# Second feed-forward and MLP with 128-column weight blocks as the stationary operand

## The chip, the core and the metric

The kernel runs on one core of a Trainium2 chip. The metric is the device time of one execution in microseconds; the median of several runs is given. A core has five engines that run their own instruction queues in order: TensorE (PE in the profile, with its weight loads as PEld), VectorE (DVE), ScalarE (ACT), GpSimd (POOL) and SyncE (SP), and 16 DMA engines.

## The reference

Two blocks of a transformer follow each other, on 256 tokens of 1024 features, in fp32. The part that the change touches is the gated feed-forward of the first block's second layer and the MLP of the second block:

```python
def swiglu(h, w_in, w_out):                 # D_FF = 2816
    g, u = jnp.split(h @ w_in, 2, axis=-1)
    return (jax.nn.silu(g) * u) @ w_out

x = layer_norm(ALPHA * x + g2 * swiglu(modulate(x, sh2, sc2), ffn_w_in[i], ffn_w_out[i]), ...)
...
h2 = rms_norm(x, norm_mlp[i])               # D_FF_2 = 4096
x = x + jnp.square(jax.nn.relu(h2 @ w_up[i])) @ w_down[i]
ple_gate = jax.nn.sigmoid(rms_norm(x, norm_ple[i]) @ w_ple_gate[i])
x = x + ple_gate * (p[i] @ w_ple[i])
```

## The kernel before

Tokens stand in two halves (t = 0, 1) of 128. Products are made from fp32 numbers that are split in two fp32r parts: hi is the number rounded to fp32r, lo the rest; a product is hi·hi + hi·lo + lo·hi. The transposed activations of a stage stand in `xTh` (hi) and `xTl` (lo), 128 features by 8 k by 256 tokens.

All weights come as tiles of 128 x 1024 in the order of one list (`make_plan`). SP issues one DMA per tile into a ring of 11 raw tiles. `Stream.split` turns a raw tile into hi (ACT, L285) and lo (DVE, L291). Eight split tiles can be held. `st.done(key)` gives a tile back and `pump` then issues the next split, as long as fewer than 7 are held; `st.get` of a tile that isn't split yet issues it in any case, as the eighth. Each engine's instructions run in the order in which the program issues them (`manual_schedule`), so where a split, an evacuation or a norm is issued sets its place in its engine's queue.

The layer's second feed-forward, `ffn(1, ...)`, takes its 2816 inner columns in chunks of 512 (one of 256): for each chunk and half, `do_g` and `do_u` multiply with the activations as the stationary operand and 512 weight columns moving (`mmN`, L376 to L378), into a PSUM tile of `mmt()`; ACT applies Silu (L961), DVE multiplies (L969). `tr` transposes the result in 128 x 128 pieces on PE (L981), because the output product needs the inner features on the partitions, and `split_evac` makes hh (ACT, L425) and hl (DVE, L426) of it. `o` multiplies these with the O weights into `ops_[t]` (`mmK`, L390 and L392; the last chunk in `mmK_tail`, L403 to L405). The MLP does the same with `up`, `trm` (L1603) and `down`, ReLU on ACT (L1595) and the square on DVE (L1596), in 8 chunks of 512.

At the start of a phase only the first token half is ready. In the feed-forward `x1_ready` is called within `do_u(0, 0)`: it transposes s[1] (L722), ACT scales it per feature in 128-column pieces (L745) and splits it (L425, L426). In the MLP `rx_t(1, ...)` is called behind `up(0, 0)`: L722, then eight scalings on ACT (L736) and eight on DVE (L738). Both chains begin with a norm that is issued ahead of the phase (`ln_core`, L890; `rms_core`, L1214 to L1219). At the end of a phase `after0` or `rcore(0)` computes the norm of half 0 while PE still multiplies for half 1, and in the MLP `rx_t(0, ...)` transposes it ahead of the last 24 matmuls. `mid` holds steps of the next stage (rows, modulation columns) that are issued within the chunks.

PSUM tiles: two each of `mmt`, `trt` (one bank) and `big` (two banks).

Of the kernel before, what the change touches and what calls it, by code (L numbers as in the profile page):

```python
# [10 lines left out]
F32R = mybir.dt.float32r  # L11
# [7 lines left out]
P = 128  # L19
# [44 lines left out]
UPM = 8  # L64
# [12 lines left out]
def nblocks(key, src, row0, rows, col0, width):  # L77
    per = BW // width
    return [("w", key + (i,), src, row0 + i * per * P, per, col0, width) for i in range(rows // (per * P))]


def make_plan():
# [43 lines left out]
    f1 = ffn(1)  # L126
# [13 lines left out]
    prev = []  # L140
    for j in range(DMLP // 512):
        plan += nblocks(("UP", j), ("w_up_2", 0), 0, D, 512 * j, 512) + prev
        prev = [("w", ("DN", j, i), ("w_down_2", 0), 512 * j + i * P, 1, 0, 1024) for i in range(4)]
    plan += prev
# [27 lines left out]
def body(ctx: ExitStack, tc: tile.TileContext, wst, prm, cst, cst2, poolp, xT_d, cT_d, x_d, head, lam_d,  # L172
# [51 lines left out]
    xTh = cp.t([P, KD, T], "xTh", F32R)  # L224
    xTl = cp.t([P, KD, T], "xTl", F32R)
# [184 lines left out]
    def xlh(t):  # L410
        return lambda k: (xTh[:, k, t * P:(t + 1) * P], xTl[:, k, t * P:(t + 1) * P])

# [729 lines left out]

    pps = [big()]
# [95 lines left out]
    ffn(1, fp, x_t(1), ac1(0), lambda: None, after1_1, {XM: mid_xa, 4: mid1_c, 5: mid_g2r})  # L1239
# [345 lines left out]
    J = DMLP // 512  # L1585
    hs, hT = {}, {}
    ops_ = [big(), big()]

    def up(j, t, mid={}):
        ps = mmt()  # L1590
        mmN(ps, xlh(t), mkey(("UP", j), 4), mid=mid)
        if t == 1:
            st.done(*mkey(("UP", j), 4))
        h = fp.t([P, 512], f"h{t}", bufs=2)
        A.activation(h, ps, AF.Relu)  # L1595
        V.tensor_tensor(h, h, h, op=OP.mult)  # L1596
        hs[j, t] = h

    def trm(j, t):
        h = hs.pop((j, t))  # L1600
        ps = trt()
        for i in range(4):
            TE.transpose(ps[:, i * P:(i + 1) * P], h[:, i * P:(i + 1) * P], ident)  # L1603
        hh = fp.t([P, 4, P], f"hh{t}", F32R, bufs=2)
        hl = fp.t([P, 4, P], f"hl{t}", F32R, bufs=2)
        split_evac(ps.rearrange("p (k t) -> p k t", t=P), hh, hl)
        hT[j, t] = (hh, hl)

    def down(j, t, done):
        hh, hl = hT.pop((j, t))  # L1610
        if j == J - 1:
            keys = [("DN", j, i) for i in range(4)]
            mmK_tail(halves(ops_[t]), [(hh[:, i], hl[:, i]) for i in range(4)], keys)
# [5 lines left out]
        for i in range(4):  # L1619
            mmK(halves(ops_[t]), (hh[:, i], hl[:, i]), ("DN", j, i), j == 0 and i == 0, False)  # L1620
            if done:
                st.done(("DN", j, i))
# [147 lines left out]
```

## Time and profile before

| | |
|---|---|
| median of 3 runs | 1156.6 us (1154.83 to 1158.38) |
| profiled execution | 1158.82 us, its span 1156.8 us |
| mean granted clock of TensorE | 0.993 |
| PE busy | 1116.0 us (96%), 5186 matmuls |
| DVE, ACT busy | 760.6 us (66%), 558.8 us (48%) |
| weight splits | 316 on ACT (1056 ns) and 316 on DVE (1220 ns) |
| HBM read | 232.6 MB, 202 GB/s over the span |

The span is the time from the first to the last instruction of the profiled execution; the 2.0 us by which its own time is longer lie around it. Matmuls are pipelined and their ends are modelled, so the duration of one (some 390 ns for 512 columns) is longer than the distance between the starts of two. A time in brackets behind an instruction is idle time of its engine just before it, with what ended it.

### The profile page before, as it was taken

The numbers are of one execution on the slowest core, as the hardware profiler recorded it, in microseconds if no ns is written. First come the engines' busy times: TensorE is split into PE (matmuls) and PEld (weight loads), VectorE is DVE, ScalarE is ACT, GpSimd is POOL, SyncE is SP. The second block draws the span as 40 slices with busy tenths as digits, with TensorE's granted clock in tenths as the row PEclk, the third lists the DMA queues.
The fourth block names the chain that finished last, engine by engine and source line by source line (L and its number), as shares of the span: only waits on it lengthen the run. The fifth ranks groups of instructions, "written<-read, shape, count | busy, mean of one in ns | idle before, by whom it ended". The sixth has DMA issues, their size and how long they took to land. (4 is left out here: it accounts for less than half of the span.)

```text
span 1156.8 us, 14163 instructions
## 1 busy us (share of the span) xinstructions
PE 1116.0 (96%) x5186; PEld 881.8 (76%) x5186; DVE 760.6 (66%) x1114; ACT 558.8 (48%) x913; POOL 22.7 (2%) x35
## 2 busy tenths in 40 slices
PE   7999888999999999999999999999999999999998
PEld 3578665678888776888887787886777877888887
DVE  7984967669986875677346765455545785555465
ACT  3452456454444527544444755457235374445353
POOL 0000000000000000000000110000000000000000
PEclk9999989999999999999999999999999999999999
DMA  9972742569997915668563755444344645464611
GB/s 360 351 274 102 273 145 66 196 236 357 354 419 286 336 58 203 218 225 300 170 231 119 241 188 180 146 164 153 102 146 130 216 151 195 166 210 163 206 38 37
DMA packets 65922, 234.62 MB, mean 203 GB/s; under 512 B 7323, under 2 KB 8347, under 8 KB 65852
## 3 DMA queue, kind: packets, MB, share of 16 engines
q1 hardware_dynamic: 64080, 227.97, 55.7%
q10 hardware_dynamic: 1772, 5.74, 1.5%
q8 instruction: 41, 0.67, 0.2%
q14 instruction: 29, 0.24, 0.1%
HBM read 232.63 MB, written 1.05 MB: 202 GB/s over the span
## 5 line engine op out<-in xcount | busy, mean ns | idle before, releaser
L291 DVE TENSOR_TENSOR lo<-raw,hi 128x1024 fp32r<-128x1024 f32 x316 | 375.2, 1220 | 139.8 <-ACT hi L285 136.1
L285 ACT ACTIVATE hi<-raw 128x1024 fp32r<-128x1024 f32 x316 | 322.5, 1056 | 82.9 <-PE mm L378 60.9
L376 PE MATMUL mm<-hi,xTh 128*128 128x512 f32 (+1 forms) x872 | 337.6, 387 | 4.0 <-ACT xTh L425 2.7
L377 PE MATMUL mm<-lo,xTh 128*128 128x512 f32 (+1 forms) x872 | 331.8, 380 | 2.0 <-DVE lo L291 1.3
L378 PE MATMUL mm<-hi,xTl 128*128 128x512 f32 (+1 forms) x872 | 332.2, 381 | 0.6 <-DVE xTl L738 0.4
L376 PEld LDWEIGHTS mm<-hi,xTh 128*128 128x128 f32 x872 | 164.1, 188 | 40.8 <-issue 4.7
L378 PEld LDWEIGHTS mm<-hi,xTl 128*128 128x128 f32 x872 | 164.0, 188 | 34.0 <-DVE xTl L426 1.9
L377 PEld LDWEIGHTS mm<-lo,xTh 128*128 128x128 f32 x872 | 164.2, 188 | 33.5 <-DVE lo L291 3.6
L269 DVE SCALAR_TENSOR_TENSOR raw<-raw,crow 128x1024 f32<-128x1024 f32 x80 | 96.7, 1218 | 0.0
L390 PE MATMUL big<-hi,hh 128*128 128x512 f32 x256 | 80.6, 396 | 0.0
L390 PE MATMUL big<-lo,hh 128*128 128x512 f32 x256 | 79.2, 391 | 0.0
L392 PE MATMUL big<-hi,hl 128*128 128x512 f32 x256 | 79.0, 390 | 0.0
L425 ACT ACTIVATE hh<-tr 128x512 fp32r<-128x512 f32 (+1 forms) x40 | 23.0, 576 | 97.4 <-PE tr L981 54.8
L961 ACT ACTIVATE h<-mm 128x512 f32<-128x512 f32 (+1 forms) x24 | 13.5, 561 | 90.2 <-PE mm L378 90.2
L426 DVE TENSOR_TENSOR hl<-tr,hh 128x512 fp32r<-128x512 f32 (+1 forms) x40 | 26.3, 661 | 46.3 <-ACT hh L425 45.6
L392 PEld LDWEIGHTS big<-hi,hl 128*128 128x128 f32 x256 | 48.1, 188 | 10.4
L390 PEld LDWEIGHTS big<-lo,hh 128*128 128x128 f32 x256 | 48.0, 188 | 10.3
L390 PEld LDWEIGHTS big<-hi,hh 128*128 128x128 f32 x256 | 46.7, 188 | 8.6
L420 POOL TENSOR_TENSOR st<-st,half 128x4 f32<-128x4 f32 (+1 forms) x28 | 21.8, 778 | 1036.8 <-DVE st L418 1023.6
L1596 DVE TENSOR_TENSOR h<-h 128x512 f32<-128x512 f32 x16 | 11.0, 688 | 33.6 <-ACT h L1595 33.5
L1595 ACT ACTIVATE h<-mm 128x512 f32<-128x512 f32 x16 | 9.6, 599 | 38.0 <-PE mm L378 38.0
L667 ACT ACTIVATE p<-big,st 128x512 f32<-128x512 f32 x16 | 11.0, 689 | 31.7 <-DVE st L666 31.7
(316 smaller groups left out, 1261.5 us busy)
## 6 DMA issues: line engine op xcount, KB each, us to landing
raw<-in_dram SPq DMA_DIRECT2D x426, 512.0 KB, 5.0
row<-in_dram ACTq DMA_DIRECT2D x8, 512.0 KB, 6.4
tok<-in_dram SPq DMA_DIRECT2D x8, 256.0 KB, 7.5
xa<-in_dram SPq DMA_DIRECT2D x2, 512.0 KB, 5.7
out_dram<-sg SPq DMA_DIRECT2D x3, 256.0 KB, 2.0
pmat<-in_dram ACTq DMA_DIRECT2D x1, 544.0 KB
crow<-in_dram ACTq DMA_DIRECT2D x1, 512.0 KB, 6.8
out_dram<-sg SPq DMA_DIRECT2D x2, 128.0 KB, 1.7
```

The lines of the kernel that those rows point to most:

```text
L269: V.scalar_tensor_tensor(raw, raw, 1.0, crow, op0=OP.mult, op1=OP.mult, accum_out=mc[l][:, nb:nb + 1])
L285: A.activation(hi, raw, AF.Copy)
L291: V.tensor_tensor(lo, raw, hi.bitcast(F32), op=OP.subtract)
L376: TE.matmul(ps, h, hi[:, sl], start=s, stop=False)
L377: TE.matmul(ps, h, lo[:, sl], start=False, stop=False)
L378: TE.matmul(ps, l, hi[:, sl], start=False, stop=e)
L390: TE.matmul(halves[f], h, w[:, f * 512:(f + 1) * 512], start=first and b == 0, stop=False)
L392: TE.matmul(halves[f], l, hi[:, f * 512:(f + 1) * 512], start=False, stop=last)
L420: G.tensor_tensor(r, v, half_e[:, :w], op=OP.pow)
L425: A.activation(dh, ps, AF.Copy)
L426: V.tensor_tensor(dl, ps, dh.bitcast(F32), op=OP.subtract)
L961: A.activation(h[:, :w], ps[:, :w], AF.Silu)
```

## The change

Weight blocks of 128 inner columns become the stationary operand and the activations move, so that the inner activations come out with features on the partitions. `xTh` and `xTl` become one tile `xT4` in which, for each k, the 256 tokens of hi lie beside those of lo. `ws_mm` issues per k one matmul of the hi weights on both parts (512 columns) and one of the lo weights on the hi part (256 columns) into the lo half of the PSUM tile; `ws_sum` adds the two halves (a copy on ACT, an addition on DVE). The transposes are gone; `split_evac` now reads the result from SBUF. `ws_order` writes out the order: the first 3 blocks (feed-forward) or 4 (MLP) run for token half 0, then x1 is called, then they run for half 1; all later blocks run for both halves at once, and output products follow at least two blocks (lag) behind, except that the last 7 blocks' products for half 1 are kept for the end. The four last blocks' products are in `tail`. `ws_plan` lists the weight tiles in the order of use, and the three steps of `mid` move to blocks 6, 16 and 19 of 22.

```diff
--- before.py
+++ after.py
@@ -61,7 +61,7 @@
 XR = (6, 6)
 MQ = 6
 BA = 6
-UPM = 8
+WM = (6, 16, 19)
 F32K = (0, 1, 2, 3, 4)
 VM = (1, 1, 1, 1, 0, 0, 0, 0)
 EN = (0, 2, 0)
@@ -77,6 +77,35 @@
 def nblocks(key, src, row0, rows, col0, width):
     per = BW // width
     return [("w", key + (i,), src, row0 + i * per * P, per, col0, width) for i in range(rows // (per * P))]
+
+
+def ws_order(n, n0, lag, keep_):
+
+    seq = [("in", i, 0) for i in range(n0)] + [("x1", 0, 0)] + [("in", i, 1) for i in range(n0)]
+    q = 0
+    for i in range(n0, n):
+        seq.append(("in", i, None))
+        while q <= min(i - lag, n - 6):
+            seq += [("out", q, t) for t in range(1 if q >= n - keep_ else 2)]
+            q += 1
+    seq += [("out", i, 0) for i in range(q, n - 4)] + [("tail", n - 4, 0), ("a0", 0, 0)]
+    seq += [("out", i, 1) for i in range(n - keep_, n - 4)] + [("m1", 0, 0), ("tail", n - 4, 1), ("a1", 0, 0)]
+    return seq
+
+
+WS_F = (DFF // P, 3, 2, 7)
+WS_M = (DMLP // P, 4, 2, 7)
+
+
+def ws_plan(order, ins, outs):
+    plan, seen = [], set()
+    for kind, i, t in ws_order(*order):
+        fs = {"in": [ins(i)], "out": [[outs(i)]], "tail": [[outs(j) for j in range(i, i + 4)]]}.get(kind, [])
+        for b in sum(fs, []):
+            if b[1] not in seen:
+                seen.add(b[1])
+                plan.append(b)
+    return plan
 
 
 def make_plan():
@@ -123,7 +152,8 @@
     f0 = ffn(0)
     plan += f0[:W0] + weave(f0[W0:W1], rest[24 - NV + NAT:]) + f0[W1:]
     plan += [("p", ("PW", b), ("pool_w", 0), 2 * b) for b in range(2)]
-    f1 = ffn(1)
+    f1 = ws_plan(WS_F, lambda i: [("w", (c, 1, i), ("ffn_w_in", 1), 0, KD, o_ + i * P, P) for c, o_ in (("G", 0), ("U", DFF))],
+                 lambda i: ("w", ("O", 1, i), ("ffn_w_out", 1), i * P, 1, 0, 1024))
     ple = [("t", ("PT",), "p_2")] + [("w", ("PLE", k), ("w_ple_2", 0), k * P, 1, 0, 1024) for k in range(2)]
     plan += f1[:W2] + weave(f1[W2:W3], [("m", 1, nb) for nb in range(40, 48)]) + f1[W3:] + ple
     for c in U_ORDER:
@@ -137,11 +167,8 @@
     for c in range(2):
         plan += nblocks(("ba", c), ("w_branch_a_2", 0), 0, D, 512 * c, 512)
     plan += [("w", ("W2", k), ("w_out_2", 0), k * P, 1, 0, 1024) for k in range(KD)]
-    prev = []
-    for j in range(DMLP // 512):
-        plan += nblocks(("UP", j), ("w_up_2", 0), 0, D, 512 * j, 512) + prev
-        prev = [("w", ("DN", j, i), ("w_down_2", 0), 512 * j + i * P, 1, 0, 1024) for i in range(4)]
-    plan += prev
+    plan += ws_plan(WS_M, lambda i: [("w", ("UP", i), ("w_up_2", 0), 0, KD, i * P, P)],
+                    lambda i: ("w", ("DN", i), ("w_down_2", 0), i * P, 1, 0, 1024))
     for c in range(2):
         plan += nblocks(("PG", c), ("w_ple_gate_2", 0), 0, D, 512 * c, 512)
     return plan
@@ -221,8 +248,8 @@
     prm_s = cp.t([P, PRM_W], "prm")
     mc = [cp.t([P, 48], f"mc{l}") for l in range(2)]
     half_e = cp.t([P, 184], "half")[:, :8]
-    xTh = cp.t([P, KD, T], "xTh", F32R)
-    xTl = cp.t([P, KD, T], "xTl", F32R)
+    xT4 = cp.t([P, KD, 2, T], "xT", F32R)
+    xTh, xTl = xT4[:, :, 0], xT4[:, :, 1]
     cst_s = cp.t([P, CST_W], "cst")
     crow = cp.t([P, D], "crow")
     raw0 = rg.t([P, 368], "pad")
@@ -409,6 +436,55 @@
 
     def xlh(t):
         return lambda k: (xTh[:, k, t * P:(t + 1) * P], xTl[:, k, t * P:(t + 1) * P])
+
+    def ws_mm(ps, key, t):
+        t0, tn = (0, T) if t is None else (t * P, P)
+        pv = ps[:, :2 * tn].rearrange("p (s t) -> p s t", s=2)
+        hi, lo = st.get(key)
+        for k in range(KD):
+            sl = slice(k * P, (k + 1) * P)
+            TE.matmul(pv, hi[:, sl], xT4[:, k, :, t0:t0 + tn], start=k == 0, stop=False, skip_group_check=True)
+            TE.matmul(pv[:, 1], lo[:, sl], xT4[:, k, 0, t0:t0 + tn], start=False, stop=k == KD - 1,
+                      skip_group_check=True)
+        if t != 0:
+            st.done(key)
+        return pv
+
+    def ws_sum(pool, pv, tag):
+        o = pool.t([P, T], tag, bufs=3)[:, :pv.shape[2]]
+        A.activation(o, pv[:, 1], AF.Copy)
+        V.tensor_tensor(o, pv[:, 0], o, op=OP.add)
+        return o
+
+    def ws_phase(pool, order, block, okey, ops_, x1, a0, m1, a1, mid={}):
+        hT = {}
+
+        def out(i, t):
+            hh, hl = hT[i]
+            return (hh[:, t * P:(t + 1) * P], hl[:, t * P:(t + 1) * P])
+
+        for kind, i, t in ws_order(*order):
+            if kind == "in":
+                h = block(i, t)
+                if t != 1:
+                    hT[i] = [pool.t([P, T], f"hT{c}", F32R, bufs=9) for c in "hl"]
+                sl = slice(0, T) if t is None else slice(t * P, (t + 1) * P)
+                split_evac(h, hT[i][0][:, sl], hT[i][1][:, sl])
+                if i in mid and t != 0:
+                    mid[i]()
+            elif kind == "out":
+                mmK(halves(ops_[t]), out(i, t), okey(i), i == 0, False)
+                if t:
+                    st.done(okey(i))
+            elif kind == "tail":
+                keys = [okey(j) for j in range(i, i + 4)]
+                mmK_tail(halves(ops_[t]), [out(j, t) for j in range(i, i + 4)], keys)
+                if t:
+                    st.done(keys[0])
+                    st.hold = True
+                    st.done(*keys[1:])
+            else:
+                {"x1": x1, "a0": lambda: a0(ops_[0]), "m1": m1, "a1": lambda: a1(ops_[1])}[kind]()
 
     def mkey(k, n):
         return [k + (i,) for i in range(n)]
@@ -1140,6 +1216,8 @@
     ffn(0, fp, x_t(1), ac0(0), mid_pool, ac0(1), {XM: mid_xa, 2: mid_g2c, 3: mid_g2r, 4: mid_gb, 5: mid_gbr})
 
 
+    fp.close()
+    fp = Pool("fp1")
     pps = [big()]
 
     def res(t):
@@ -1236,7 +1314,17 @@
         st.done(("PT",), ("PLE", 0), ("PLE", 1))
         ac1(1, EN)(ps)
 
-    ffn(1, fp, x_t(1), ac1(0), lambda: None, after1_1, {XM: mid_xa, 4: mid1_c, 5: mid_g2r})
+    def glu(i, t):
+        g = ws_sum(fp, ws_mm(mmt(), ("G", 1, i), t), "hg")
+        A.activation(g, g, AF.Silu)
+        u = ws_sum(fp, ws_mm(trt(), ("U", 1, i), t), "hu")
+        V.tensor_tensor(u, u, g, op=OP.mult)
+        return u
+
+    ws_phase(fp, WS_F, glu, lambda i: ("O", 1, i), [big(), big()], x_t(1), ac1(0), lambda: None, after1_1,
+             {WM[0]: mid_xa, WM[1]: mid1_c, WM[2]: mid_g2r})
+    st.hold = False
+    st.pump()
 
 
     hx.clear()
@@ -1582,69 +1670,14 @@
     fp = Pool("fp3")
 
 
-    J = DMLP // 512
...
-            rcore(1)(ops_[1])
+    def relu2(i, t):
+        z = ws_sum(fp, ws_mm(mmt() if i % 2 else trt(), ("UP", i), t), "hz")
+        h = fp.t([P, T], "hg", bufs=3)[:, :z.shape[1]]
+        V.scalar_tensor_tensor(h, z, 0.0, z, op0=OP.max, op1=OP.mult)
+        return h
+
+    ws_phase(fp, WS_M, relu2, lambda i: ("DN", i), [big(), big()], lambda: rx_t(1, prmc("nmlp")), rcore(0),
+             lambda: rx_t(0, prmc("nple")), rcore(1))
 
 
     st.hold = False
```

## Rows read from the trace of the kernel before

**Rows 1.** Windows: busy of PE, PEld, DVE, ACT, POOL; clock, DMA share, GB/s

```profile
442.30:632.76 190.46, 188.98 (x903) 157.08 (x904) 110.60 (x129) 88.18 (x114) 1.63 (x3) 1.00 0.59 204
...
941.80:1128.86 187.06, 184.62 (x849) 151.98 (x848) 105.11 (x123) 89.06 (x119) 1.09 (x2) 1.00 0.48 163
```

**Rows 2.** Timeline, start and duration in us: first, last of 24 512-column matmuls

```profile
1128.86 0.39 PE L376 MATMUL mm<-hi,xTh 128*128 128x512 f32 x1
...
1134.08 0.40 PE L378 MATMUL mm<-hi,xTl 128*128 128x512 f32 x1
```

**Rows 3.** The same view: first and last of 24 matmuls of 256 columns

```profile
534.86 0.28 PE L377 MATMUL mm<-lo,xTh 128*128 128x256 f32 x1
...
537.60 0.28 PE L376 MATMUL mm<-hi,xTh 128*128 128x256 f32 x1
```

**Rows 4.** The same view: eight transposes and the second matmul behind them

```profile
1122.54 1.03 PE L722 MATMUL tr<-cst,s 128*128 128x128 f32 x8
...
1123.64 0.40 PE L404 MATMUL big<-lo,hh 128*128 128x512 f32 x1
```

**Rows 5.** Groups by line, both phases: xcount | busy us, mean ns | idle

```profile
L981 PE MATMUL tr<-cst,h 128*128 128x128 f32 x44 | 6.8, 273 | 0.2 <-ACT row L775 0.2
...
L1603 PE MATMUL tr<-cst,h 128*128 128x128 f32 x64 | 9.6, 272 | 1.3 <-DVE h L1596 1.3
```

**Rows 6.** Timeline of all engines at the start of the MLP

```profile
941.80 0.39 PE L376 MATMUL mm<-hi,xTh 128*128 128x512 f32 x1
...
946.15 0.75 DVE L1219 TENSOR_SCALAR s<-xa,st 128x1024 f32<-128x1024 f32 x1 [0.67 <-POOL st L420]
...
946.82 1.22 DVE L291 TENSOR_TENSOR lo<-raw,hi 128x1024 fp32r<-128x1024 f32 x1
...
948.01 2.17 ACT L736 ACTIVATE xTh<-tr,prm 128x128 fp32r<-128x128 f32 x8
...
948.43 0.50 PE L376 MATMUL mm<-hi,xTh 128*128 128x512 f32 x1 [0.15 <-ACT xTh L736]
...
949.19 2.16 DVE L738 SCALAR_TENSOR_TENSOR xTl<-tr,prm,xTh 128x128 fp32r<-128x128 f32 x8 [0.34 <-ACT xTh L736]
...
949.59 0.19 PEld L378 LDWEIGHTS mm<-hi,xTl 128*128 128x128 f32 x1 [0.86 <-DVE xTl L738]
```

**Rows 7.** Groups by line, whole span: operations of 128 and 256 columns

```profile
L1284 ACT ACTIVATE jk<-mm 128x128 f32<-128x128 f32 x32 | 8.4, 283 | 0.0
...
L1329 DVE SCALAR_TENSOR_TENSOR sc<-c2d,mm 128x128 f32<-128x128 f32 x8 | 1.7, 280 | 5.4 <-PE mm L1325 5.4
...
L969 DVE TENSOR_TENSOR h<-h,mm 128x256 f32<-128x256 f32 x4 | 1.7, 418 | 1.1 <-PE mm L378 1.1
```

**Rows 8.** Timeline at the start of the second feed-forward

```profile
440.08 1.51 ACT L745 ACTIVATE tev<-tr,Bc,Gc 128x128 f32<-128x128 f32 x4 [0.79 <-PE tr L722]
...
442.49 0.68 DVE L426 TENSOR_TENSOR xTl<-tev,xTh 128x512 fp32r<-128x512 f32 x1
...
444.35 0.69 DVE L426 TENSOR_TENSOR xTl<-tev,xTh 128x512 fp32r<-128x512 f32 x1 [1.18 <-ACT xTh L425]
...
449.84 0.82 DVE L890 TENSOR_SCALAR s<-s,st,st 128x1024 f32<-128x1024 f32 x1 [0.66 <-POOL st L420]
...
454.60 0.63 ACT L425 ACTIVATE xTh<-tev 128x512 fp32r<-128x512 f32 x1
...
455.26 0.69 DVE L426 TENSOR_TENSOR xTl<-tev,xTh 128x512 fp32r<-128x512 f32 x1 [3.47 <-ACT xTh L425]
```

**Rows 9.** Windows around a fall of the clock (columns as in group 1)

```profile
820.80:824.20 3.40, 1.96 (x11) 1.24 (x12) 3.00 (x5) 1.06 (x1) 0.00 (x0) 1.00 0.93 308
...
824.20:827.60 3.40, 3.40 (x10) 2.19 (x9) 1.39 (x3) 0.00 (x0) 0.00 (x0) 0.50 0.37 147
```

**Rows 10.** Groups by line, MLP: the last product's matmul on lo weights

```profile
L404 PE MATMUL big<-lo,hh 128*128 128x512 f32 x16 | 6.4, 397 | 0.6 <-DVE lo L291 0.6
```

**Rows 11.** Groups by line, MLP: weight loads

```profile
L377 PEld LDWEIGHTS mm<-lo,xTh 128*128 128x128 f32 x128 | 24.1, 188 | 4.8
```

More of the change, by code (lines that the diff above doesn't have):

```diff
@@ L1582, in body @@
     fp = Pool("fp3")
-    J = DMLP // 512
[L1586 to L1613, printed above, removed]
-            if done:
-                st.done(*keys[:2])
-                st.hold = True
-                st.done(*keys[2:])
-            return
[L1619 to L1622, printed above, removed]
@@ L1624, in body @@
-    up(0, 0, {UPM: lambda: rx_t(1, prmc("nmlp"))})
-    if UPM == 8:
-        rx_t(1, prmc("nmlp"))
-    up(0, 1)
-    trm(0, 0)
-    trm(0, 1)
-    for j in range(1, J):
-        up(j, 0)
-        up(j, 1)
-        if j < J - 1:
-            down(j - 1, 0, False)
-            trm(j, 0)
-            down(j - 1, 1, True)
-            trm(j, 1)
-        else:
-            trm(j, 0)
-            down(j - 1, 0, False)
-            trm(j, 1)
-            down(j, 0, False)
-            rcore(0)(ops_[0])
-            down(j - 1, 1, True)
-            rx_t(0, prmc("nple"))
-            down(j, 1, True)
-            rcore(1)(ops_[1])
+    def relu2(i, t):
[3 more added lines that the diff above has]
+        return h
```

## The prediction

> **What bounds the kernel now.** I read first the busy time of each engine in the two stretches that the change rewrites: the second feed-forward (442.3 to 632.8 us) and the MLP (941.8 to 1128.9 us). TensorE is busy for 189.0 of 190.5 us and for 184.6 of 187.1 us, at a granted clock of 1.00 (2.4 GHz); VectorE and ScalarE stand at 46 to 58%, the DMA engines at 48 to 59% [rows 1]. So an instruction saved on TensorE is time saved, as long as nothing else comes late. The busy figures overlap, so I price matmuls by the distance of their starts. In the timeline 24 matmuls of 512 moving columns start from 1128.86 to 1134.08, 0.227 us apart [rows 2]; 24 of 256 columns from 534.86 to 537.60, 0.119 us apart, so half the columns cost 6 ns more than half the time [rows 3]. From eight transposes at 1122.54 to the second matmul behind them at 1123.64 it is 1.10 us; less 0.227 for the first matmul, 0.109 each [rows 4]. Last I read the starts of both phases, where PE waits for the normalised second token half.
>
> **Matmuls.** Both versions split each product into hi·hi, lo·hi and hi·lo. Before, a 512-column weight block costs 3 matmuls of 512 per token half and k. Now one 128-column block costs per k a pair: hi weights with 512 moving columns (xh and xl side by side), lo weights with 256. The down and O products keep their matmuls. Blocks: 22 for each of G and U, 32 for UP, 8 k each, so 352 + 256 = 608 pairs. Those of the first 3 (FFN) and 4 (MLP) blocks run once per token half, with 256 and 128 columns: 3·2·2·8 = 96 and 4·2·8 = 64 half pairs, 160 in all. The other 304 + 224 = 528 run whole.
> - Transposes gone: 44 and 64 [rows 5], 108 × 0.109 = -11.8 us.
> - Before, the pairs' columns cost 1.5 × 0.227 = 0.3405 us. The 256-wide chunk, 96 × 0.120 = 11.5 instead of 32 × 0.3405 = 10.9, was dearer: -0.6.
> - 528 whole pairs: 0.227 + 0.120 = 0.347, +0.0065 each: +3.4.
> - 160 half pairs: 0.120 + L against 0.170, where L is the 128-column fp32r matmul with fresh weights that the trace does not have. Below: the line through 512 and 256 columns gives 0.067 (+2.7 in all). Above: the 512-column price 0.227 (+28.3). I take 0.109, the transposes' row: they are fp32 and not fp32r, but they too move 128 columns, each with 128 fresh weight columns [rows 4]. That is +9.4.
>
> The Trainium skill (TensorE: Matmul & The Clock Gate, section LDWEIGHTS) says that a load lasts its column count divided by 1.2 ns, 107 ns for 128 columns. By it L would be no less than 0.107 and the half pairs cost +9.1; by the line alone they cost +2.7. No row above undercuts it.
>
> Sum on TensorE: -11.8 - 0.6 + 3.4 + 9.4 = +0.4 us (-6.3 with L at 0.067). The change then stands or falls with its waits.
>
> **The start of the MLP.** PE starts up(0,0) at 941.80; the RMS chain of token half 1 ends on DVE with L1219 (946.15), behind it one weight split (L291, 946.82, until 948.04); PE transposes, L736 on ACT runs eight scalings from 948.01, L738 on DVE eight from 949.19, and PE, which had started at 948.43, waits until 949.59 [rows 6]; the transposes of the first h wait 1.3 us for DVE [rows 5]. Idle there: about 1.2 + 1.4 = 2.6 us.
> After, four narrow blocks run over token half 0 before x1 calls rx_t(1): 32 × 0.229 = 7.3 us, to 949.1. But each queues a chain of its own ahead of x1: ACT copy, DVE add, DVE relu-square, ACT hh, DVE hl. Queues are kept in program order, and the next block's copy stands behind this block's hh, its add behind this block's hl. So blocks don't overlap: one costs two ACT and two DVE operations of 0.28 us [rows 7] with hops of 0.03 (L425 ends at 455.23, L426 starts at 455.26 [rows 8]), some 1.24 us. None of the adds can start before 948.04, since L1219 and the split stand ahead on DVE. The last hh ends at 948.04 + 4 × 1.24 - 0.3 = 952.7. Only then do the four L736 of the first half run (1.2 us), then the four L738 (1.1 us) that also free the transposes' PSUM buffer, which in(0,1) takes: PE goes on at 955.1. From 941.8 to there it worked 7.3 + 0.9 us, idle 5.1. The wait for h goes, since out(0) comes only behind in(4). Idle: 5.1 against 2.6, +2.5 us. Bounds: 0 (no chain) to +4 (a split between two blocks).
>
> **The start of the feed-forward.** The same, with eight operations per block (copy, add, Silu, copy, add, multiply, hh, hl), seven of them in series, some 2.1 us. DVE is held by the layer norm until 450.6 (L890, 449.84) [rows 8]. Three blocks end their hh at 456.8; the matmuls end at 455.2. The feature modulation of x1 takes 3.1 us from the first L745 to the end of the first xTl (440.08 to 443.18) and 5.0 us to the second (445.04) [rows 8]. So token half 1 starts at 459.9 and waits again at its k = 4 until 461.8. The first matmul of the phase also needs xTl at once (443.2 instead of 442.3), since hi weights now meet xh and xl in one matmul. Idle from 442.3 until three blocks are done for both halves (471.8): 29.5 - 96 × 0.229 - 0.9 = 6.6 us; before, the whole phase has 190.5 - 189.0 = 1.5 us [rows 1]. +5.1 us, between 0 and +7.
>
> **The clock.** PE would stand nearly still for about 3.9 us (951.2 to 955.1) and 3.3 us (456.6 to 459.9). Before, the stretch 820.8 to 824.2, with 1.96 us busy, is followed by one at 0.50 (1.2 GHz) [rows 9]. If that happens at a start, 3.4 us run at half speed: 0 to 1.7 us each. I take half: +1.7 for both.
>
> **The rest.** At each end one wait for a split of the eighth, forced weight tile (0.6 us idle in each phase) [rows 10]: seven tiles are held now, so -0.6 each, or 0. In the tail, 18 instead of 24 matmuls cover the RMS chain of half 0 (4.1 instead of 5.4 us), and one more PG split lands behind it: 0 to +1.5. I take -0.6. The steady middle is hidden: per MLP block PE needs 8 × 0.347 + 12 × 0.227 = 5.5 us, DVE two splits of 1.22 and three 256-column operations of 0.42 [rows 7], 3.7 us, and a block's activations are wanted only two blocks later. If that cover failed, some 0.5 us of each of 28 MLP blocks, 14 us, would show. Splits behind a done() follow the block's matmuls on ACT and DVE; the chain is queued behind them, and only out() waits for it. The three steps moved inside the feed-forward (mid_xa to block 6, mid1_c with its two row DMAs on ACT's queue to 16, mid_g2r with its 8 transposes to 19) issue what they issued before; mid_xa is four DVE operations of a split's size, 4.9 us in a row, hidden by the two blocks between in(i) and out(i) (2 × 8.3 us), and up to 4.9 us if they weren't. SP's stream keeps the number of its tiles.
>
> **Sum.** 0.4 + 2.5 + 5.1 + 1.7 - 0.6 = +9.1 us. The profiled execution took 1158.8 us (span 1156.8, 2.0 around it); such a one would take 1167.9. The median shown is 2.2 us lower, 1156.6, so the forecast is 1165.7.
>
> **Rivals.**
> - *The cover holds (about the same).* If the early blocks' chains kept up with PE, the +7.6 of the starts and the +1.7 of the clock would fall away: 0.4 - 0.6, 1156.4 us. For it: x1 is called after 7 to 11 us of matmuls, as before. Against: the adds can't start before 948.04 and 450.6.
> - *Narrow matmuls follow the line (faster).* L = 0.067 and the cover holds: -6.3 - 0.6, 1149.7 us. The place is the 160 half pairs; below L = 0.088 (PE sum -2.9, with -0.6 at -3.5) it is faster by over 0.3%. With the chains as I count them, cheap narrow matmuls gain only where PE doesn't wait, the second token half, about 3 us: 1162.
> - *Narrow matmuls are as dear as wide ones.* L = 0.227: +18.9 more, of which some 4 lie in the starts' waits: 1180 us.
> - *A 256-column matmul can't hide its successor's load.* The loads show 0.188 us each [rows 11]; a whole pair would be 0.227 + 0.188, +0.068 each: 528 × 0.068 = +36, 1202 us. Against it speaks that 256-column matmuls with a fresh load each run 0.119 apart [rows 3].
> - *It doesn't do what it says:* no place found; the transposes and their reads leave the code.
>
> **How the numbers follow.** Forecast 0.55 (own range 1159 to 1173), cover holds 0.19, line 0.13, dear narrow 0.09, load exposed 0.04. From 1150 to 1175 lie the first three; the last two, 0.13, and the edges stay out. A measurement of this kernel tells about 0.3% (3.5 us) from no change: below 1153 faster (0.13); same 0.19 plus 0.06 of the forecast's low end, 0.25; slower 0.62.
>
> **What would show it.** In the timeline of after: starts 0.227 and 0.120 apart in whole pairs; 0.12 + L in half pairs; no transposes between in and out; PE idle before in(0,1) in both phases, released by L738 or by xTl; the granted clock behind it. Wrong if the adds of the first blocks run before 948 and 450, if L is near 0.067, or if PE waits in the middle of a phase.

## The result and the profile after

| | before | after |
|---|---|---|
| median (before: the three runs and a fourth) | 1156.99 us | 1186.47 us (1184.13 to 1190.86) |
| ratio | | 1.0261, 95% interval 1.0227 to 1.0295 |
| span of the profiled execution | 1156.8 us | 1184.4 us |
| mean granted clock of TensorE | 0.993 | 0.981 |
| matmuls, PE busy | 5186, 1116.0 us | 5494, 1130.3 us |

The change costs 29.5 us. The forecast was slower, but by 9.1 us, with 1175 as its upper end. To see where the rest went I cut both executions at the last product of the first feed-forward, of the second, of the W2 stage and of the MLP, and sorted PE's time between: *waits* (start-to-start distances above 0.6 us, less 0.25 for the matmul itself), *half clock* (half of the time at a granted clock of 0.5, without the waits in it) and the rest, which is PE at full speed. The end counts to PE's last matmul.

| stage | before | after | waits | half clock | rest |
|---|---|---|---|---|---|
| pool stage and second feed-forward | 212.3 | 233.5 | +8.9 | +9.4 | +3.0 |
| GLA to W2 (not changed) | 309.3 | 311.9 | +1.8 | +1.5 | -0.7 |
| MLP | 187.1 | 191.4 | +1.9 | +2.7 | -0.2 |
| end | 23.8 | 24.7 | +0.9 | 0 | -0.1 |
| sum | | +29.1 | +13.5 | +13.6 | +2.0 |

Ahead of the first cut, where the code is the same, the profiled execution of after is 1.6 us shorter, so the spans differ by 27.6. The matmuls themselves cost little, 2 us. Waits and the slow clock behind them cost 27 us, two thirds of it in the feed-forward. The windows of after first, as in [rows 1]: the two phases, then the four stretches at 0.5 (1.2 GHz) in them that the kernel before does not have.

```profile
443.00:652.30 209.30, 199.91 (x1072) 173.49 (x1072) 132.20 (x202) 101.74 (x183) 1.63 (x3) 0.95 0.56 183
964.00:1155.30 191.30, 186.88 (x978) 159.37 (x977) 126.27 (x198) 94.65 (x159) 1.09 (x2) 0.98 0.49 160
443.20:450.00 6.80, 6.51 (x31) 6.52 (x31) 4.03 (x8) 4.28 (x9) 0.54 (x1) 0.50 0.80 279
460.30:467.10 6.80, 5.99 (x27) 5.80 (x28) 2.97 (x5) 4.45 (x9) 0.00 (x0) 0.50 0.21 63
620.70:627.50 6.80, 6.05 (x21) 5.28 (x22) 2.77 (x5) 2.33 (x4) 0.00 (x0) 0.50 0.39 116
975.70:982.50 6.80, 5.38 (x25) 5.41 (x26) 4.17 (x12) 3.10 (x9) 0.00 (x0) 0.50 0.26 77
```

Each is 6.8 us long and PE works for 5.4 to 6.5 us of it, so some 3 us are lost in each, about as much as in the waits of 3.0 to 3.8 us ahead of three of them; the one ahead of the fall at 620.7 is 6.1 us long. What PE waited for, from the view of waits (total, times, longest):

```profile
PE mm L446 <- DVE xT L502: 6.3, 3, 2.8
PE tr L850 <- DVE hu L456: 5.8, 1, 5.8
PE tr L446 <- DVE xT L814: 3.5, 1, 3.5
```

The first are the starts of the feed-forward (for the split of the activations of each half), the third the second half's start in the MLP (for its scalings; L738 before). The second is new and stands in the middle of the feed-forward. Its timeline:

```profile
614.93 0.28 PE L447 MATMUL tr<-xT,lo 128*128 128x256 f32 x1
615.05 0.62 PE L850 MATMUL tr<-cst,mcol 128*128 128x128 f32 x4
...
617.99 0.42 DVE L456 TENSOR_TENSOR hg<-mm,hg 128x256 f32<-128x256 f32 x1
...
619.84 1.23 DVE L318 TENSOR_TENSOR lo<-raw,hi 128x1024 fp32r<-128x1024 f32 x1 [1.43 <-ACT hi L312]
620.98 0.42 DVE L456 TENSOR_TENSOR hu<-tr,hu 128x256 f32<-128x256 f32 x1
621.45 0.90 PE L850 MATMUL tr<-cst,mcol 128*128 128x128 f32 x3 [5.79 <-DVE hu L456]
```

PE's last matmul of block 19's U product (L447) starts at 614.93 and ends at 615.2, but DVE adds it up only at 620.98 (L456): ACT and DVE work 5.8 us behind PE. In the two engines' queues, G's evacuation (hg) and the splits, hi on ACT (L312) and then lo on DVE (L318), stand ahead of that addition, in an order that makes each engine wait for the other (DVE 1.43 us for hi). Behind U, PE has the eight transposes of mid_g2r (L850). They use the `trt` pool, two buffers, which now also takes U's products. The first four find a buffer free; the next four need the one that U still occupies.

Now the pairs, in the same view: first those of a half block, then those of a whole one:

```profile
452.09 0.34 PE L446 MATMUL tr<-xT,hi 128*128 128x256 f32 x1
452.26 0.22 PE L447 MATMUL tr<-xT,lo 128*128 128x128 f32 x1
452.32 0.33 PE L446 MATMUL tr<-xT,hi 128*128 128x256 f32 x1
...
589.77 0.40 PE L446 MATMUL tr<-xT,hi 128*128 128x512 f32 x1
590.01 0.28 PE L447 MATMUL tr<-xT,lo 128*128 128x256 f32 x1
590.13 0.40 PE L446 MATMUL tr<-xT,hi 128*128 128x512 f32 x1
```

By the medians over the whole trace the steps are 0.236 and 0.117 (528 whole pairs, 0.353 in sum) and 0.172 and 0.060 (160 half pairs, 0.232). Last, the timeline where the MLP takes up the second token half, from the norm (L1297) on:

```profile
968.44 0.75 DVE L1297 TENSOR_SCALAR s<-xa,st 128x1024 f32<-128x1024 f32 x1 [0.67 <-POOL st L496]
969.11 1.22 DVE L318 TENSOR_TENSOR lo<-raw,hi 128x1024 fp32r<-128x1024 f32 x1
970.25 0.28 DVE L456 TENSOR_TENSOR hz<-tr,hz 128x128 f32<-128x128 f32 x1
971.44 0.28 DVE L456 TENSOR_TENSOR hz<-mm,hz 128x128 f32<-128x128 f32 x1
...
972.97 0.66 PE L798 MATMUL tr<-cst,s 128*128 128x128 f32 x4 [0.92 <-DVE hz L456]
973.83 0.28 DVE L456 TENSOR_TENSOR hz<-mm,hz 128x128 f32<-128x128 f32 x1
...
975.85 2.16 DVE L814 SCALAR_TENSOR_TENSOR xT<-tr,prm,xT 128x128 fp32r<-128x128 f32 x8 [0.74 <-ACT xT L812]
977.12 0.55 PE L446 MATMUL tr<-xT,hi 128*128 128x256 f32 x1 [3.49 <-DVE xT L814]
```

The four chains stand 1.19 us apart, none of them before the norm and the split, and behind the last come the scalings. This is the queue that the prediction drew.

### The profile page after: what moved, and what is told of

It is laid out like the page before. It is cut to its first block, busy times and chain, and to the rows that moved or that the text cites. A ratio compares the mean times of both kernels' runs of the same rounds, so it can differ in the third digit from the quotient of the medians.

```text
span 1184.4 us, 15048 instructions
## 1 busy us (share of the span) xinstructions
PE 1130.3 (95%) x5494; PEld 907.1 (77%) x5494; DVE 807.1 (68%) x1266; ACT 582.5 (49%) x1029; POOL 22.7 (2%) x35
## 4 chain that ended last, share of the span: by engine, by line
PE 65%; DVE 17%; ACT 8%; issue 4%; DMA 4%; POOL 0%; SPq 0%; ACTq 0%; DVEq 0%; POOLq 0%
PE mm L403 10%; PE mm L405 10%; PE mm L404 10%; PE big L417 9%; DVE lo L318 6%; PE big L419 5%; DMA raw<-in_dram 4%; PE tr L446 4%; PE mm L446 4%; ACT hi L312 4%; DVE junkb L602 2%; DVE raw L296 2%; PE mm L447 2%; PE tr L447 2%; PE big L411 1%
## 5 line engine op out<-in xcount | busy, mean ns | idle before, releaser
L318 DVE TENSOR_TENSOR lo<-raw,hi 128x1024 fp32r<-128x1024 f32 x316 | 378.5, 1222 | 151.7 <-ACT hi L312 149.1
L312 ACT ACTIVATE hi<-raw 128x1024 fp32r<-128x1024 f32 x316 | 323.9, 1054 | 65.5 <-PE mm L405 49.0
L403 PE MATMUL mm<-hi,xT 128*128 128x512 f32 (+1 forms) x552 | 215.4, 390 | 1.6 <-ACT mv L1465 1.2
L404 PE MATMUL mm<-lo,xT 128*128 128x512 f32 (+1 forms) x552 | 210.9, 382 | 2.9 <-DVE lo L318 2.9
L405 PE MATMUL mm<-hi,xT 128*128 128x512 f32 (+1 forms) x552 | 211.0, 382 | 0.0
L446 PE MATMUL mm<-xT,hi 128*128 128x512 f32 (+1 forms) x344 | 120.4, 400 | 6.4 <-DVE xT L502 6.3
L403 PEld LDWEIGHTS mm<-hi,xT 128*128 128x128 f32 x552 | 104.2, 189 | 26.9 <-issue 4.7
L404 PEld LDWEIGHTS mm<-lo,xT 128*128 128x128 f32 x552 | 104.3, 189 | 23.6 <-DVE lo L318 4.5
L446 PE MATMUL tr<-xT,hi 128*128 128x512 f32 (+1 forms) x344 | 118.4, 395 | 3.5 <-DVE xT L814 3.5
L405 PEld LDWEIGHTS mm<-hi,xT 128*128 128x128 f32 x552 | 104.1, 189 | 21.0 <-DVE xT L502 0.9
L296 DVE SCALAR_TENSOR_TENSOR raw<-raw,crow 128x1024 f32<-128x1024 f32 x80 | 96.8, 1219 | 0.0
L447 PE MATMUL mm<-xT,lo 128*128 128x256 f32 (+1 forms) x344 | 94.5, 275 | 0.0
L447 PE MATMUL tr<-xT,lo 128*128 128x256 f32 (+1 forms) x344 | 93.6, 272 | 0.0
L446 PEld LDWEIGHTS mm<-xT,hi 128*128 128x128 f32 x344 | 68.6, 199 | 19.3 <-DVE xT L502 7.2
L447 PEld LDWEIGHTS mm<-xT,lo 128*128 128x128 f32 x344 | 69.0, 201 | 1.1
L447 PEld LDWEIGHTS tr<-xT,lo 128*128 128x128 f32 x344 | 68.2, 198 | 0.5
```

The costliest lines, as they stand in the source:

```text
L296: V.scalar_tensor_tensor(raw, raw, 1.0, crow, op0=OP.mult, op1=OP.mult, accum_out=mc[l][:, nb:nb + 1])
L312: A.activation(hi, raw, AF.Copy)
L318: V.tensor_tensor(lo, raw, hi.bitcast(F32), op=OP.subtract)
L403: TE.matmul(ps, h, hi[:, sl], start=s, stop=False)
L404: TE.matmul(ps, h, lo[:, sl], start=False, stop=False)
L405: TE.matmul(ps, l, hi[:, sl], start=False, stop=e)
```

## The experiments

Ratios are against the kernel before on the same chip, at 1156.5 to 1157.3 us. "Theory Q" is the reading above: queues on ACT and DVE, and the clock that falls behind the waits; rival P of the first two runs is that the pairs and half pairs are dear in themselves, so that the cost goes by their number.

**One part at a time.** The feed-forward alone, and the MLP alone:

```diff
-    plan += ws_plan(WS_M, ...)                    # e1: the MLP's loop and plan as before
-    f1 = ws_plan(WS_F, ...)                       # e2: the feed-forward's as before
```

> Only the second feed-forward is changed; the MLP is that of the kernel before. Theory Q (queues and clock: the excess of 29.5 us is waits of PE at the starts and at block 19, and stretches at half clock behind them): the last product of the feed-forward ended 21 us later in the trace of after than in that of before, and the stage behind it lost 2.6 us, so 1179 us, give or take 2. Rival P (price: the pairs and half pairs themselves are dear): the cost goes by their number, 352 of 608, 17 us: 1174 us.

> Only the MLP is changed. Theory Q: the MLP lost 4.4 us and the stage behind it 0.9 in the trace of after: 1162 us, give or take 2. Rival P: 256 of 608 pairs, 12.5 us: 1169 us. Either way this and e1 should add up to the full change.

Measured: 1179.05 us (1.0195, 1.0177 to 1.0214) and 1162.53 us (1.0057, 1.004 to 1.0074), as theory Q had them; P's 1174 and 1169 lie outside the two intervals. The parts add up: 22.6 + 6.1 = 28.7 of 29.5 us. In the run with the MLP alone there is one fall of the clock in this phase, behind the 3.8 us wait of its start:

```profile
950.40:957.20 6.80, 6.70 (x31) 6.73 (x32) 3.76 (x9) 2.30 (x4) 0.00 (x0) 0.50 0.25 80
```

**The splits ahead of the evacuation.** `ws_mm` gives the weight tile back, and so queues the next split, before its product is evacuated. Here it does so afterwards:

```diff
-        if t != 0:
-            st.done(key)
         return pv
...
         g = ws_sum(fp, ws_mm(mmt(), ("G", 1, i), t), "hg")
+        if t != 0:
+            st.done(("G", 1, i))
...                                                # likewise for U, and for UP in the MLP
```

> The full change, but the weight tile of an in product is given back behind the sum of its PSUM halves instead of ahead of it, so that the split of the next tile stands behind the copy and the addition in the queues of ACT and DVE, not ahead of them. Theory Q: the evacuation chain of the feed-forward, 7.6 us a block now, falls under 6.5 us, its lag behind PE at block 19 falls from 5.8 us to under 2, and the 6.1 us wait of the row transposes there and the half clock behind it go: -9 us, 1177.5 us. Rival: the row transposes wait for the modulation columns or a DMA, the wait stays: 1186 us.

Measured: 1179.59 us (1.0199, 1.017 to 1.0229); the four runs lie at 1176.8 to 1182.8, and the profiled one is among the shorter. Of the wait at block 19, 0.6 us is left, and the fall behind it is gone; this window holds the place of both, at full clock:

```profile
605.00:622.00 17.00, 16.44 (x96) 14.17 (x95) 9.71 (x15) 9.33 (x18) 0.00 (x0) 1.00 0.44 144
```

The feed-forward is 8.2 us shorter than in after. Not all of that is the order's: the first fall lasted 3.4 us here and 6.8 in after. Against the run with the feed-forward alone, which has the same first two falls, it is 6.6 us. The MLP is 1.7 us longer: there the give-back now puts a split between a block's sum and its square, the last block's square starts behind one (L318 on DVE, 1129.74 to 1130.97), and the tail waits 1.3 us for it. So the 5.8 us lag has a cause in the order of the queue, and the order has a price elsewhere.

**What made the lag grow.** The same wait, from the other side: mid_xa, four operations of DVE, moved behind mid_g2r.

```diff
-WM = (6, 16, 19)
+WM = (20, 16, 19)
```

> The changed kernel with mid_xa, four operations of DVE of 1.2 us each, moved inside the feed-forward from block 6 to block 20, behind mid_g2r. Theory X (the lag of the evacuation behind PE, 5.8 us at block 19, is for the most part those 4.9 us, which DVE has not caught up by then): PE's wait of 6.06 us ahead of the fifth transpose of mid_g2r falls to about 1.2, the fall of the clock behind it goes, the feed-forward gains 5 to 8 us less what mid_xa costs at its end (0 to 2): 1180 us. Rival S (the lag comes from the splits queued ahead of the evacuations, whatever else DVE has to do): the wait stays near 6 and the time at 1186.5 us.

Measured: 1185.65 us (1.0252, 1.0234 to 1.0271). The wait at block 19 falls to 0.9 us as theory X has it, yet almost nothing is gained: the time is rival S's (1186.5), not X's (1180). The timeline from there to the tail:

```profile
614.80 0.43 PE L850 MATMUL tr<-cst,mcol 128*128 128x128 f32 x2 [0.90 <-DVE hu L456]
...
623.49 1.22 DVE L986 SCALAR_TENSOR_TENSOR xa<-s,row 128x1024 f32<-128x1024 f32 x1
...
627.14 1.23 DVE L988 SCALAR_TENSOR_TENSOR xa<-row,xa 128x1024 f32<-128x1024 f32 x1
...
629.42 0.42 DVE L456 TENSOR_TENSOR hg<-mm,hg 128x256 f32<-128x256 f32 x1
...
633.78 0.79 PE L430 MATMUL big<-hi,hTh 128*128 128x512 f32 x1 [3.49 <-ACT hTh L501]
```

The four operations (L986 and L988, twice) now stand ahead of the evacuation of block 21, so the tail (L430) waits 3.5 us for its activations, and the clock falls there instead, as the window shows:

```profile
632.70:639.50 6.80, 5.72 (x14) 4.47 (x15) 0.97 (x3) 0.42 (x1) 0.00 (x0) 0.50 0.24 77
```

DVE must spend the 4.9 us somewhere, and at neither of the two places do they lie beside other work. From block 12 on the evacuation of a block recurs every 7.58 us in after (hu is added at 583.92, 591.51 and 599.09) where PE needs 8.38 (2 × 8 × 0.353 + 12 × 0.227 = 8.37), so there a delay of 4.9 would take six blocks to work off. But each of blocks 4 to 11 (from 494.7 to 560.0) also has a product for the modulation columns on DVE (L296; L269 in the kernel before, eight there too), and with it the evacuation takes 8.73 us, more than PE's 8.38:

```profile
543.71 0.42 DVE L456 TENSOR_TENSOR hu<-tr,hu 128x256 f32<-128x256 f32 x1
...
551.30 1.22 DVE L296 SCALAR_TENSOR_TENSOR raw<-raw,crow 128x1024 f32<-128x1024 f32 x1
...
552.44 0.42 DVE L456 TENSOR_TENSOR hu<-tr,hu 128x256 f32<-128x256 f32 x1
```

So in after the lag of U's addition behind PE goes from 4.45 us at block 6 to 8.96 at block 7 (mid_xa), grows by 0.34 a block to 10.33 at block 11 and is 5.77 at block 19. In this run it is 4.52, 4.86, 6.23 and 0.86: at block 19 the two differ by the whole 4.9 us of mid_xa.

**The clock by itself.** Matmuls whose result nobody reads, put into the three waits at the starts, so that PE does not stand:

```diff
+    keep(4)                                       # ahead of the feed-forward; 2 in the second run
     ws_phase(fp, WS_F, glu, ...
-        ... x_t(1), ac1(0), ...
+        ... lambda: (x_t(1)(), keep(5)), ac1(0), ...              # 3 in the second run
+        for _ in range(8):                        # behind rx_t(1) in the MLP; 4 in the second run
+            TE.matmul(mops[0][:, 0:512], crow[:, 0:P], crow[:, 0:512], start=True, stop=True)
```

> The full change with dummy matmuls of 512 columns in three of PE's gaps: 4 ahead of the feed-forward's first block, 5 behind its x1, 8 behind the MLP's x1; nothing is left out. Theory Q: the gaps stay, but PE isn't still in them, and three stretches of 6.8 us at 1.2 GHz (from 443.2, 460.3 and 975.7 us) go: 3.4 + 3.0 + 2.7 = -9 us, 1177.5 us, up to 1 us more if a dummy outlasts its gap. Rival: the gaps alone are the cost and the low clock lies in idle time: 1186 us or more.

Measured: 1182.55 us (1.0226, 1.0209 to 1.0243), 5 us behind the expectation. The falls at the feed-forward's start and in the MLP were gone, of the one behind x1 3.4 us were left, but the fillers (`keep(n)` issues n of them) outlasted the waits that they were to fill; the eight of the MLP, in a wait of 3.8 us:

```profile
968.77 7.03 PE L1685 MATMUL big<-crow 128*128 128x512 f32 x16
```

So again with fewer:

> The changed kernel with matmuls whose result nobody reads, in the three starts where PE stood before its clock fell: 2 ahead of the feed-forward, 3 behind the transposes of its second token half, 4 behind those of the MLP's. At 0.86 us each (the run before with fillers: 7.03 us for 8) they end before the waits do (3.0, 3.1 and 3.8 us). Theory C (a fall to half clock costs what PE works in it, about 3 us each, ahead of every later wait): the three falls go, 1186.5 - 9 = 1177.5 us. Rival I (the time lost at half clock is given back at the next wait, the 6.06 us at block 19 in the feed-forward and none in the MLP): the feed-forward stays at +21, the MLP gains 3, 1183.5 us. Rival O (fillers take the place of the wait and delay the first products): 1186 us.

Measured: 1176.28 us (1.0171, 1.0152 to 1.019); 10.2 us less than after, where theory C said 9. Windows of the three starts:

```profile
441.90:448.70 6.80, 6.21 (x54) 6.06 (x54) 4.28 (x7) 4.54 (x9) 0.54 (x1) 1.00 0.82 304
459.00:465.80 6.80, 6.80 (x50) 5.81 (x50) 3.37 (x6) 2.42 (x5) 0.00 (x0) 0.96 0.24 77
968.00:982.00 14.00, 13.95 (x90) 11.42 (x91) 9.49 (x25) 7.62 (x21) 0.00 (x0) 1.00 0.28 84
```

Nothing of the kernel's own work was changed; the clock stayed up (50 to 54 matmuls in 6.8 us where after has 27 to 31). But only 5.8 of the 7.6 us by which the spans of the profiled executions differ lie in the two phases, 3.3 in the feed-forward and 2.5 in the MLP; the rest, and the 10.2 of the medians with it, holds differences in stages that weren't changed. In the MLP the 2.5 us are the price of its fall almost to the number (2.7). In the feed-forward 2.7 us are gained between the first product of the second half and block 3, where the second fall had cost 3.0, but only 0.4 ahead of it. There a shorter fall of 3.4 us remained (456.2 to 459.6), and the three fillers behind x1 ran at half clock and held PE until 460.0, although the first activations were ready at 457.4:

```profile
456.04 4.54 PE L243 MATMUL tr<-crow 128*128 128x512 f32 x6 [1.40 <-ACT tev L821]
```

So the price of the second fall and of the MLP's is shown, some 3 us each; that of the first, and of the one at block 19, is argued from the half clock alone.

**Both causes together**, the late give-back in the feed-forward alone and the fewer fillers:

> As the kernel with 2, 3 and 4 fillers, and in the feed-forward the weight block is given back (and the next split queued) behind the evacuation of its product, not ahead of it. Theory Q (the lag of the evacuation behind PE and the clock are separate causes): the 8.4 us that the late give-back gained in the feed-forward come on top of the 9 of the fillers, 1186.5 - 17.4 = 1169 us, and what is left above the kernel before, 12.5 us, is PE's own matmuls (+4.1) and the waits at the starts. Rival (both take away the same lost time, since a start at full clock leaves the evacuation as late): 1177 us.

Measured: 1173.38 us (1.0137, 1.0112 to 1.0163), not 1169. In the feed-forward they add up nearly in full: 7.3 us on top of the fillers, 10.7 left above the kernel before. Of the 4 us that are missing, 3.4 stand in the profiled execution in the stage between, which is 4.9 us longer than before's (in the run with fillers alone 1.5): the clock falls there twice. Why it does so is open; it is not a property of the kernel, for its four executions range from 1168.74 us (mean granted clock 0.998) to 1174.78 (0.993, the profiled one).

```profile
793.90:800.70 6.80, 6.80 (x15) 4.46 (x14) 0.69 (x1) 6.68 (x9) 0.00 (x0) 0.50 0.09 36
838.20:841.60 3.40, 3.40 (x10) 2.64 (x9) 1.08 (x3) 0.00 (x0) 0.00 (x0) 0.50 0.27 106
```

**The queue at the MLP's start.** The four products of the first half are kept in four PSUM banks (two of them the output's, still free) and evacuated behind x1:

```diff
             if kind == "in":
-                h = block(i, t)
+                if early and t == 0:
+                    pend.append((i, early[0](i, ops_)))
+                    continue
...
+                if kind == "x1" and early:
+                    x1()
+                    for i, pv in pend:
+                        fin(i, 0, early[1](pv))
```

> The changed kernel; at the start of the MLP alone the four products of the first token half are kept in four PSUM banks and evacuated behind the transposes and scalings of the second half, not ahead of them. Theory Q (the scalings of x1 stand behind four chains on ACT and DVE): PE's wait of 3.76 us ahead of the second half falls to about 1.2 (the scalings alone), the fall of the clock behind it goes, MLP -6, 1180.5 us. Rival R (the wait is x1's own: the RMS chain, transposes, scalings and their splits): it stays above 3 us, 1186 us. Rival L (the deferred chains make the second half's products wait for their PSUM buffers): the wait moves behind in(1,1), 1185 us.

Measured: 1181.18 us (1.0211, 1.0184 to 1.0238). That is the number of theory Q, but not by its way. The waits of 0.92 and 3.49 us become one of 2.04, and the clock falls all the same. In the timeline:

```profile
969.96 2.16 DVE L824 SCALAR_TENSOR_TENSOR xT<-tr,prm,xT 128x128 fp32r<-128x128 f32 x8 [2.94 <-ACT xT L822]
...
971.23 0.36 PE L446 MATMUL tr<-xT,hi 128*128 128x256 f32 x1 [2.04 <-ACT hz L455]
```

The profile puts the end of this wait down to a copy on ACT (L455). But the product starts 1.27 us behind the first scaling on DVE (969.96), as it does in after (975.85 to 977.12), so what is left is more likely x1's own scalings, rival R's share. The window behind it:

```profile
972.90:979.70 6.80, 6.63 (x33) 6.47 (x31) 4.38 (x14) 3.00 (x11) 0.00 (x0) 0.50 0.00 0
```

The MLP gains 1.8 us in the profile; 2.3 more come from the feed-forward, whose code is that of after: its first fall lasted 3.4 us here and not 6.8, and its wait at block 19 is 1.1 us shorter. So the time agrees with theory Q by luck. The queue ahead of x1 is confirmed as the cause of more than half of the wait (4.41 us, now 2.04); that its removal saves the fall is not.

**What bounds a pair.** Eight matmuls on hi weights, then eight on lo:

```diff
             TE.matmul(pv, hi[:, sl], xT4[:, k, :, t0:t0 + tn], start=k == 0, stop=False, ...)
+        for k in range(KD):
+            sl = slice(k * P, (k + 1) * P)
             TE.matmul(pv[:, 1], lo[:, sl], xT4[:, k, 0, t0:t0 + tn], ...)
```

> The changed kernel with another order inside each product: eight matmuls on hi weights, then eight on lo weights, in place of hi, lo, hi, lo. Theory W (each matmul waits for its own 128-column weight load, which cannot be shorter than about 0.116 us): in half pairs the eight hi go on at 0.119 and the eight lo rise from 0.060 to 0.116, the sum of a half pair stays at 0.23; whole pairs go from 0.353 to 0.346; 528 x 0.007 = -3.7, 1183 us. Rival S (what costs is the change of width or of the PSUM stretch between neighbours): half pairs 0.119 + 0.060 = 0.18, 160 x 0.05 = -8.5 besides, 1174 us. Rival N (neither): 1186.5 us.

Measured: 1182.55 us (1.0229, 1.021 to 1.0247): theory W. The half blocks, and lo and hi of a whole block:

```profile
452.31 1.17 PE L446 MATMUL mm<-xT,hi 128*128 128x256 f32 x8
453.32 1.01 PE L449 MATMUL mm<-xT,lo 128*128 128x128 f32 x8
454.16 1.17 PE L446 MATMUL tr<-xT,hi 128*128 128x256 f32 x8
...
580.50 1.12 PE L449 MATMUL mm<-xT,lo 128*128 128x256 f32 x8
581.46 2.00 PE L446 MATMUL tr<-xT,hi 128*128 128x512 f32 x8
```

From row to row: 16 matmuls of half a block take 1.85 us (452.31 to 454.16), as in after (8 × 0.232 = 1.86). By the medians the hi ones now step at 0.120 and the lo ones at 0.112, not 0.060. So the price of a half pair doesn't come from the change of width. I read it as the load of the weights: a matmul of 128 columns behind others of 128 goes no faster than its weights are loaded, and behind one of 256 columns the same time only shows at another place, the next hi. The loads (PEld) of half pairs in after fit that: they start 0.108 and 0.123 apart in turn, by the medians, where the matmuls start 0.172 and 0.060 apart.

```profile
452.14 0.19 PEld L447 LDWEIGHTS tr<-xT,lo 128*128 128x128 f32 x1
452.27 0.19 PEld L446 LDWEIGHTS tr<-xT,hi 128*128 128x128 f32 x1
452.38 0.19 PEld L447 LDWEIGHTS tr<-xT,lo 128*128 128x128 f32 x1
```

No run has narrow matmuls that keep their weights, so the load as the cause is not shown apart. Whole pairs step at 0.227 + 0.120 = 0.347, the figure of the prediction; only the alternation cost 0.006 more. The time agrees with theory W in part by luck: in the profiled executions the two phases gain 0.9 us (3.0 on PE at full speed, against it a fall of 10.3 us behind x1 where after has 6.8), the unchanged stages 3.0.

The Trainium skill (TensorE: Matmul & The Clock Gate, section LDWEIGHTS) gives a load its column count divided by 1.2 ns, 107 ns for 128 columns; the 0.112 us between the starts in this run agree with it at full clock, the 0.213 us at a granted clock of 0.5 do not.

**The steady middle alone.** If the losses lie at the starts and in the feed-forward, the kernel before should gain from the new way in the MLP from block 4 on, with the first 512 inner columns done as before:

```diff
+    plan += nblocks(("UP0",), ("w_up_2", 0), 0, D, 0, 512)
     plan += ws_plan(WS_M, lambda i: [] if i < 4 else [("w", ("UP", i), ...
...
+    def x1():
+        up0(0)                                    # as up(0, 0) before
+        rx_t(1, prmc("nmlp"))
```

> The kernel before with the new way in the MLP alone, and there from block 4 on: the first 512 columns of UP run as before (activations stationary, eight transposes), so there are no half pairs and no chains ahead of x1. Theory Q (what the change costs in the MLP lies in its start: half pairs, queue, clock): the start costs what it did before, 28 blocks cost 28 x 8 x (0.353 - 0.3405) = +2.8, 56 transposes less give 56 x 0.109 = -6.1, the end costs +0.8: -2.5 us, 1154.5 us where before is 1157. Rival (the steady middle costs too): at or above 1157 us.

> As the kernel before with the new way from block 4 of the MLP on, and with the eight matmuls on hi weights ahead of the eight on lo weights: pairs at 0.347 in place of 0.353, 28 x 8 x 0.006 = -1.4 more, -3.8 against before, 1153.2 us. Rival as for the run without the new order.

Measured: 1154.04 us (0.9979, 0.997 to 0.9988) and 1152.66 us (0.9963, 0.995 to 0.9975): 2.8 and 4.2 us less than the kernel before, where 2.5 and 3.8 were expected. The MLP of the second takes 181.9 us between the cuts of the table, before 187.1, and its clock stays up:

```profile
939.90:1121.70 181.80, 179.94 (x905) 151.99 (x904) 121.69 (x178) 93.37 (x146) 1.09 (x2) 1.00 0.52 169
```

## Why the prediction was off, point by point

| term | predicted | measured in the two traces |
|---|---|---|
| PE's matmuls | +0.4 | +2.8 (rest of both phases) |
| start of the MLP | +2.5 | +2.6 |
| start of the feed-forward | +5.1 | +3.9 |
| splits at the ends, tail | -0.6 | -0.6 |
| steps moved inside the feed-forward | 0 | +5.8 |
| clock in both phases | +1.7 | +12.1 |
| stage between | 0 | +2.6 |
| sum | +9.1 | +29.2 |

- *Starts, right in the MLP, right by number in the feed-forward.* The chain of 1.24 us per MLP block is 1.19, no add runs ahead of the norm, and idle time there is 0.94 + 3.51 = 4.45 us against 5.1 counted. The feed-forward's waits (3.02, 0.95 and 3.07 between starts) stand where I named them, released by the splits of the activations. But the queue that I drew there, "three blocks end their hh at 456.8; the matmuls end at 455.2", isn't in the trace: U of the third block is added 0.35 us behind PE (457.23), and at full clock too (0.34, with the fewer fillers). The 3.07 us are x1's own transposes, scalings and splits, in which PE has nothing else to do.
- *Clock, the failed step.* "If that happens at a start, 3.4 us run at half speed: 0 to 1.7 us each. I take half." Both the number of falls and their length were too small. There are four, where I had priced two at half their chance: behind both waits that I named, behind the waits for xTl at the feed-forward's first products (3.02 and 0.95 us), which I had counted in part among the idle time but not for the clock, and at block 19. Each is 6.8 us long, and together they cost 12.1 us where I had put 1.7. The row on which I rested is one of two falls of 3.4 us in that trace [rows 9]; a window of the same trace shows one of 6.8, of which I had read the first half alone:

```profile
158.60:165.40 6.80, 5.29 (x20) 3.75 (x20) 4.80 (x11) 5.06 (x15) 0.32 (x1) 0.50 0.68 240
```

With it as the bound (half of 5.29 us of work, 2.6), the two places that I named would have come to 5.3 us, and the feed-forward's first products to 2.6 more.
- *Moved steps, the second failed step.* "mid_xa ... hidden by the two blocks between in(i) and out(i)." That cover is for `out`, which indeed never waits. But a product's evacuation also frees its PSUM buffer, and those are two deep; the transposes of mid_g2r, which I had "issue what they issued before", ask for a buffer of the pool that the change gave to U. The bound that I wrote, "up to 4.9 us if they weren't", was of the right size (5.8), yet I took nothing of it. I had also worked out the steady load of DVE for an MLP block alone. For a feed-forward block it is three splits and four operations, 5.3 us of work, but 7.58 us with the waits between ACT and DVE in it, of PE's 8.38, and 8.73 in the blocks that also hold L296: no room for 4.9 us. My own sign of being wrong, "if PE waits in the middle of a phase", came true here.
- *Pairs.* L was the disputed price: 0.109 taken, 0.067 and 0.227 its bounds. In the order of the change it reads 0.060 and would look like the line; but the pair is 0.232 against 0.229 forecast, since the step from hi to lo is 0.172 and not 0.120. Run side by side it is 0.112. The sum was right, the place of it wasn't; and that the price of an fp32 transpose would fit an fp32r matmul was a guess that came out. For whole pairs 0.347 was forecast, 0.353 measured: 528 × 0.006 = +3.2, more than the 2.4 that PE's term was short of.
- *The stage between* was left out of the sum. A wait of 1.6 us at its beginning is new (the ple products wait for a PSUM buffer, and the scalings on DVE that free it, L814 at 656.80, stand behind four splits), and the clock falls twice instead of once, at 805 and 846.
- *The rivals.* None held. That the load can't be hidden behind 256 columns (1202 us) is refuted by 0.117; the cover did not hold. By its time alone "narrow matmuls are as dear as wide ones" (1180 us) lies nearest, but it needs half pairs of 0.120 + 0.227, and they take 0.232.

## What to carry to other kernels

The waits of 3 to 6 us that this change gave PE cost twice, once as themselves and once more as some 3 us of half speed behind each (shown with fillers for two of the four). So price a new wait with the longest fall that the trace shows, and count every wait for it, those in the middle too. When a product's evacuation takes over work that PE did, add up the chain of ACT and DVE with its waits for each other per block, beside PE's block, before calling anything hidden, and look at who else uses its PSUM buffers. A way that loses at the edges of a phase may still win in its middle: keep the old one where only half the data is there.

## What the runs showed of the hardware that I had not expected

- At a granted clock of 0.5 a pair of narrow matmuls slows nearly as much as wide ones: in after the half pair takes 0.427 us by the medians (0.320 and 0.107) against 0.232 at full clock, 1.84 times, and a whole pair 0.640 against 0.353, 1.81 times. If loads set its pace, as read above, the loads slow down with the array; their starts are 0.21 us apart there.
- A plain fp32 matmul of 512 columns, the filler, is two records of 0.43 us in the trace (x16 for eight), 0.86 us in all, nearly four times an fp32r one of the same width (0.227).
- Alternating 512 and 256 columns costs 6 ns a pair more than eight of the one and eight of the other (0.353 and 0.347), worth 1.4 us in the MLP (1154.04 to 1152.66, the two intervals overlap slightly). Width, weight tile and stretch of PSUM alternate together; which of them costs it is open.
- Kernels with the same code in a stage differ there in the number and length of the clock's falls (none to two between GLA and W2, 3.4 to 6.8 us each; in the feed-forward up to 10.3), so a stage that wasn't changed can differ by 1 to 5 us between two profiles.
